# Later attention's first q and k loaded in the decode stage; the first MLP's first block in three column ranges and its residual added to the accumulator

## The chip, the cores and the metric

The kernel runs on 1 core of one Trainium2 chip. The metric is the device time of the whole program in microseconds, as the median of several runs; lower is better.

## What is computed

One layer of a hybrid decoder on a prompt of 1024 tokens and on 8 x 4 sample tokens (32 rows), model width 1024, all in float32:

```
h   = rmsnorm(x) * (1 + scale1) + shift1
q_a, k_a, v_a, q_b, f_b, i_b, g_b = split(h @ w_in)
o_a = stick_breaking(q_a, k_a, v_a)         # 8 heads x 64, strictly causal
o_b = gated linear recurrence(q_b, f_b, i_b, g_b)
x   = x + gate1 * (concat(o_a, o_b) @ w_out)
h2  = rmsnorm(x) * (1 + scale2) + shift2
x   = x + gate2 * (relu(h2 @ w_up)**2 @ w_down)
```

Stick-breaking attention gives row t the weights sigmoid(z[t,s]) * prod over s<j<t of (1 - sigmoid(z[t,j])). The sample tokens attend to 1024 cached positions each, in pages, and carry their own recurrent state.

## The kernel before, in words

Float32 products are made of three products of rounded parts: each operand is split into a high part (a cast on ScalarE) and a low part (a subtraction on VectorE or POOL), and `stationary_weights` (L202 to L204) and the down-projection (L1219 to L1221) issue high x high, high x low and low x high into one accumulation bank. Each such product has its own 128x128 weights. A weight piece is a 512 KB load on SP's queue (L159), a cast (L149) and a subtraction (L150); two raw buffers hold the loads.

The stages, in order: the start with q; k and v; the recurrence with the attention of rows 0 to 511 beside it; the first out-projection with its norm (tiles of 128 tokens, 0 to 3); the first MLP on tokens 0 to 511, with the sample tokens' decode and then the later attention (rows 512 to 1023) beside it; the second out-projection; the second MLP.

The order in which each engine gets its instructions is written at compile time by a planner. It simulates the program with its own costs; where several instructions could go, the earlier in program order goes first, moved up by the priorities that the code sets. On the chip every engine and every queue takes its instructions in that order and waits where an input isn't there. `interleave` at the end of the kernel mixes the steps of the first MLP (weight 64) with those of decode and attention (weight 166), so that the latter come earlier in program order and are at an end of their steps about halfway through the MLP's.

The first MLP (`mlp` with n = 512) goes in eight blocks of 512 hidden columns. A block's up half makes four groups of 128 hidden columns from all 512 tokens; each group is relu'd on ScalarE, squared on VectorE, cast on ScalarE and subtracted on VectorE. Its down half adds to eight accumulators `acc` of 128 tokens x 512 columns in SBUF. In the first block the up half is cut into column ranges (`CS`), so that it can start on tokens 0 to 255 while tiles 2 and 3 are still in the norm of the out-projection; ranges below column 256 use four banks (`M0`), the others two. Tile 3's norm ends with PE transposes (L314), scaling on ScalarE (L319), a cast on VectorE (L328) and a subtraction, whose second half POOL does (L329).

In the last block each piece of the down half is finished as follows: a residual tile `xres` (2 buffers, 256 KB) is loaded on SP's queue (L1231), POOL multiplies the accumulator by the gate `g2b` (L1232) and adds it to the residual (L1233), VectorE multiplies the last product by the gate (L1235) and adds it (L1236), and SP writes the result (L1237).

The decode reads 128 pages of 256 KB on SP's queue (L609 and cv's), transposes the keys on PE (L625), and at its end writes `mixs` (L691). The sample tokens' recurrence runs beside its second half; its step on PE (L996) reads kts (L988). `attention` loads for every head qh and ql (L881), kk (L882) and vhl (L884) on POOL's queue, from scratch in DRAM that is written long before. Its pool opens where the decode's pool closes, so its tiles take the addresses of the decode's. Per 128 rows: score products (L895, L896), two sigmoids (L899, L900), causal masks on POOL (L903, L904), a reversed running product on VectorE (L909), a product on POOL (L910), transposes on PE (L922), a split, and the products with v (L931, L932); at the end tv (L934, L935), written to DRAM (L936).

The second out-projection begins with products of the sample rows and the raw weights of w_out (L1097), which SP loads (L1111, L159).

Of the kernel before, what the change touches and what calls it, by code (L numbers as in the profile page):

```python
# [20 lines left out]
P = 128  # L21
# [22 lines left out]
RE = 0  # L44
CS = ((256,),(256,))
BF = dict(m="012345", y="67")
# [33 lines left out]
def hymba_step(ctx, tc, x_p, x_s, ck, cv, st_in, ptab, c_p, c_s, w_ada, b_ada, n1g, n2g, w_in,  # L80
# [787 lines left out]

    def attention(pb, ms, nbe):

        q0, nq, nk = 256 * ms[0], 256 * len(ms), 256 * (ms[-1] + 1)
        both = lambda t, part, p, r, cs: qkd[t, part, p, r, cs].unsqueeze(0).to_broadcast([2, 64, cs.stop - cs.start])
        for p in range(4):
            for hh in range(2):
                h = 2 * p + hh
                hr = slice(64 * hh, 64 * hh + 64)

                qh, ql = (pb.tile([P, nq], F32R, name=name, bufs=2) for name in ("qh", "ql"))
                kk_ = pb.tile([P, nk], F32R, name="kk", bufs=2)
                for part, tile_ in enumerate((qh, ql)):  # L880
                    G.dma_start(tile_, both(0, part, p, hr, slice(q0, q0 + nq)))  # L881
                G.dma_start(kk_, qkd[1, :, p, hr, 0:nk])  # L882
                vhl = pb.tile([P, nk // P, P], F32R, name="vhl", bufs=2)
# [285 lines left out]
    def mlp(h_hi, h_lo, t0, chunks, fp, nx, side=iter(())):  # L1169
# [5 lines left out]
        if n > 512:  # L1175
            res_s = fp.tile([NS, D], F32, name="res_s")
            nc.sync.dma_start(res_s, x1d[T:TA, :])
        else:
            g2b = fp.tile([P, D], F32, name="g2b")
        acc = [lp.tile([P, HW], F32, name=f"acc{c}", tag="acc", bufs=8) for c in range(KT)]  # L1180
        for blk in range(NBLK):
            u_hi, u_lo, ws = [], [], []
            cuts = (0,) + CS[t0 > 0] + (n,)
            parts = [slice(*x) for x in zip(cuts, cuts[1:])] if blk == 0 else chunks
# [9 lines left out]
            for m in range(NK):  # L1194
                ws.append(piece([wview(w_up, 0, KT, blk * FB_ + m * P, P)], KT, P, G if m in GL else V))
                u_hi.append(lp.tile([P, HW], F32R, name=f"uh{m}", tag="u", bufs=8))
                u_lo.append(lp.tile([P, HW], F32R, name=f"ul{m}", tag="u", bufs=8))
                if blk:
                    for cs in parts:
                        up(m, cs)  # L1200
                    next(side, None)
                    yield
            if blk == 0:
                for cs in parts:
                    for m in range(NK):
                        up(m, cs)
                    yield
            if n == 512 and blk == NBLK - 1:
                nc.sync.dma_start(g2b, g2d.to_broadcast([P, D]))
            for half_ in range(2) if n == 512 else ():  # L1210
# [3 lines left out]
                for tt in range(4):  # L1214
# [8 lines left out]
                    with tc.high_priority(offset=PV):  # L1223
# [4 lines left out]
                        else:  # L1228

                            xr = fp.tile([P, 512], F32, name="xres", tag="xres", bufs=nx)  # L1230
                            nc.sync.dma_start(xr, x1d[ts, cc])  # L1231
                            G.tensor_tensor(aa, aa, g2b[:, cc], op=mult)  # L1232
                            G.tensor_tensor(xr, xr, aa, op=add)  # L1233
                            yy = lp.tile([P, 512], F32, name="yy", tag="rr", bufs=2)
                            V.tensor_tensor(yy, pm, g2b[:, cc], op=mult)  # L1235
                            V.tensor_tensor(xr, xr, yy, op=add)  # L1236
                            nc.sync.dma_start(y_p[ts, cc], xr)  # L1237
                    if tt % 2:
# [56 lines left out]
    def decode_and_attention():  # L1295
        banks.update(BD)
        with ExitStack() as es:
            gd = decode(pool("decode", stack=es))
# [6 lines left out]
        with ExitStack() as es:  # L1305
            yield from attention(pool("attn1", stack=es), (2, 3), NBE)

# [59 lines left out]
```

## Time and profile before

| | |
|---|---|
| median of 3 runs | 1575.45 us (1572.76 to 1577.44) |
| the profiled execution | 1573.13 us |
| its span | 1571.4 us, 26224 instructions |
| PE busy | 1522.4 us, 97% |
| VectorE, ScalarE, POOL busy | 980.1, 623.9, 356.2 us |
| mean granted clock of PE | 0.988 |
| DMA | 223.14 MB, mean 142 GB/s |

The span is the time from the first to the last instruction of one profiled execution; the rows of the trace count from its start. The granted clock is a share of 2.4 GHz. A number in brackets behind a row of a timeline is the time for which the engine sat idle before it, and what ended that. PE is the product engine, PEld its weight loads, DVE VectorE, ACT ScalarE, SPq the queue of SP.

### The profile page before, as it was taken

What the parts mean: (1) busy time and instruction counts of PE and PEld (TensorE: products, weight loads), DVE (VectorE), ACT (ScalarE), POOL (GpSimd) and SP (SyncE); (2) the same over time, 40 slices, a digit from 0 to 9 for tenths busy, and PEclk for the clock granted to TensorE, in tenths of its full rate; (3) what the DMA queues carried; (4) which work ended last, traced back from release to release, by engine and by line L of the source; (5) the groups of instructions that cost most, each with busy time, mean ns of one, the idle gap of its engine ahead of it and who ended that gap; (6) DMA issues with size and microseconds to landing.
All of it is one profiled execution on the core that took longest, in us unless ns stands there. A gap on an engine that the chain in (4) does not pass through costs nothing.

```text
span 1571.4 us, 26224 instructions
## 1 busy us (share of the span) xinstructions
PE 1522.4 (97%) x9629; PEld 1276.1 (81%) x9629; DVE 980.1 (62%) x2084; ACT 623.9 (40%) x1187; POOL 356.2 (23%) x568
## 2 busy tenths in 40 slices
PE   7999999999999989999998999999899999999998
PEld 3666689998998777765566788888479999999998
DVE  4976438888866862444544977887585344444445
ACT  3742244444423453432232665655345322233330
POOL 0200125544210120000111776793110000000000
PEclk8999999999999989999998999999999999999999
DMA  9389873533124466667465374642744222322221
GB/s 327 110 282 308 259 216 67 111 65 76 50 62 143 135 193 216 204 220 248 150 153 126 98 139 99 137 117 90 234 149 146 87 89 87 94 82 86 89 82 58
DMA packets 249413, 223.14 MB, mean 142 GB/s; under 512 B 60507, under 2 KB 196259, under 8 KB 247236
## 3 DMA queue, kind: packets, MB, share of 16 engines
q1 hardware_dynamic: 186308, 199.26, 40.4%
q0 software_dynamic: 62976, 22.20, 8.4%
q8 instruction: 76, 1.25, 0.3%
q14 instruction: 53, 0.43, 0.1%
HBM read 190.14 MB, written 31.11 MB: 141 GB/s over the span
## 4 chain that ended last, share of the span: by engine, by line
PE 81%; DVE 8%; DMA 6%; issue 2%; ACT 2%; POOL 1%; SPq 0%; POOLq 0%; ACTq 0%; DVEq 0%
PE pm L202 15%; PE pm L203 15%; PE pm L204 15%; PE pm_qkv L215 3%; PE pm L1219 3%; PE pm_qkv L213 3%; PE pm_qkv L214 3%; PE pm L1221 3%; PE pm L1220 3%; PE pod L675 2%; PE ptd L625 2%; DMA wraw<-in_w_up_dram 1%; PE ptw L922 1%; DVE om L909 1%; PE pm_o L1143 1%
## 5 line engine op out<-in xcount | busy, mean ns | idle before, releaser
L202 PE MATMUL pm<-h_hi,whi 128*128 128x288 f32 (+3 forms) x1184 | 384.3, 326 | 4.9 <-DVE gg L792 1.7
L203 PE MATMUL pm<-h_lo,whi 128*128 128x288 f32 (+3 forms) x1184 | 381.9, 323 | 0.3 <-DVE h_lo L329 0.2
L204 PE MATMUL pm<-h_hi,wlo 128*128 128x288 f32 (+3 forms) x1184 | 380.9, 322 | 0.0
L149 ACT CAST whi<-wraw 128x1024 fp32r<-128x1024 f32 x160 | 167.9, 1052 | 317.9 <-PE pm L203 211.5
L150 DVE TENSOR_TENSOR wlo<-wraw,whi 128x1024 fp32r<-128x1024 f32 x144 | 185.1, 1286 | 157.5 <-ACT whi L149 151.6
L202 PEld LDWEIGHTS pm<-h_hi,whi 128*128 128x128 f32 x1184 | 223.6, 189 | 27.0 <-issue 9.8
L204 PEld LDWEIGHTS pm<-h_hi,wlo 128*128 128x128 f32 x1184 | 224.0, 189 | 10.3 <-issue 1.2
L203 PEld LDWEIGHTS pm<-h_lo,whi 128*128 128x128 f32 x1184 | 223.8, 189 | 9.6 <-DVE h_lo L329 0.9
L203 PE MATMUL pm<-ul,whi 128*128 128x256 f32 (+1 forms) x512 | 145.7, 288 | 0.0
L204 PE MATMUL pm<-uh,wlo 128*128 128x256 f32 (+1 forms) x512 | 145.5, 288 | 0.0
L202 PE MATMUL pm<-uh,whi 128*128 128x256 f32 (+1 forms) x512 | 143.7, 289 | 0.0
L909 DVE TENSOR_TENSOR_SCAN om<-om 128x128 f32<-128x128 f32 (+3 forms) x96 | 110.1, 1151 | 27.1 <-POOL om L903 18.8
L150 POOL TENSOR_TENSOR wlo<-wraw,whi 128x1024 fp32r<-128x1024 f32 x16 | 38.5, 2406 | 389.6 <-ACT whi L149 344.1
L910 POOL TENSOR_TENSOR be<-be,om 128x384 f32<-128x384 f32 (+3 forms) x96 | 100.2, 1053 | 51.5 <-DVE om L909 45.2
L1219 PE MATMUL pm<-whi,uh 128*128 128x512 f32 x256 | 106.1, 415 | 2.4 <-DVE acc L1227 2.2
L1221 PE MATMUL pm<-whi,ul 128*128 128x512 f32 x256 | 103.1, 406 | 1.6 <-DVE ul L1192 1.6
L1220 PE MATMUL pm<-wlo,uh 128*128 128x512 f32 x256 | 102.4, 401 | 0.0
L204 PEld LDWEIGHTS pm<-uh,wlo 128*128 128x128 f32 x512 | 95.9, 188 | 0.0
L203 PEld LDWEIGHTS pm<-ul,whi 128*128 128x128 f32 x512 | 95.9, 188 | 0.0
L202 PEld LDWEIGHTS pm<-uh,whi 128*128 128x128 f32 x512 | 94.6, 188 | 0.1
L1250 DVE TENSOR_TENSOR acc<-acc,pm 128x256 f32<-128x256 f32 (+1 forms) x96 | 41.0, 436 | 69.2 <-PE pm L204 69.2
L215 PE MATMUL pm_qkv<-whi,h_lo 128*128 128x512 f32 x192 | 77.6, 405 | 0.8 <-DVE h_lo L329 0.8
(354 smaller groups left out, 2860.9 us busy)
## 6 DMA issues: line engine op xcount, KB each, us to landing
wraw<-in_w_up_dram SPq DMA_DIRECT2D x64, 512.0 KB, 4.0
wraw<-in_w_down_dram SPq DMA_DIRECT2D x64, 512.0 KB, 4.8
wada<-in_w_ada_dram SPq DMA_DIRECT2D x16, 1024.0 KB, 9.1
raw<-in_cache_k_dram SPq DMA_DIRECT2D x64, 256.0 KB, 3.3
vt<-in_cache_v_dram SPq DMA_DIRECT2D x64, 256.0 KB, 3.9
wraw<-in_w_in_dram SPq DMA_DIRECT2D x24, 512.0 KB, 5.7
wa<-in_w_ada_dram SPq DMA_DIRECT2D x16, 512.0 KB, 6.4
qkd<-th SPq DMA_DIRECT2D x16, 256.0 KB, 7.1
```

The lines of the kernel that those rows point to most:

```text
L149: (V.tensor_copy if h is V else S.copy)(hi, src)
L150: (e or V).tensor_tensor(lo, src, hi.bitcast(F32), op=sub)
L202: TE.matmul(pm, w_hi[:, k, :], r_hi[k][:, cs], start=(k == 0), stop=False)
L203: TE.matmul(pm, w_hi[:, k, :], r_lo[k][:, cs], start=False, stop=False)
L204: TE.matmul(pm, w_lo[:, k, :], r_hi[k][:, cs], start=False, stop=(k == nk - 1))
L213: TE.matmul(pm, h_hi[:, k, cs], hi, start=(k == 0), stop=False)
L215: TE.matmul(pm, h_lo[:, k, cs], hi, start=False, stop=(k == KT - 1))
L909: V.tensor_tensor_scan(back, back, back, 1.0 if right is None else right[:, 0:1], op0=mult, op1=ALU.bypass)
L910: G.tensor_tensor(be[:, 0:w], be[:, 0:w], om[:, 1:w + 1], op=mult)
L1219: TE.matmul(pm, u_hi[m][:, ts], hi, start=(m == 0), stop=False)
L1220: TE.matmul(pm, u_hi[m][:, ts], lo, start=False, stop=False)
L1221: TE.matmul(pm, u_lo[m][:, ts], hi, start=False, stop=(m == NK - 1))
```

## The change

The first head's qh, ql and kk of the later attention are allocated in the pool of the first MLP, in the two buffers of the residual tiles and the one of the gate, and are loaded on POOL's queue at the start of the decode stage; vhl stays where it was. The first block of the first MLP has the column ranges 0 to 256, 256 to 384 and 384 to 512 in place of 0 to 256 and 256 to 512; the steps for the interleaving stay the same in number. In the last block the gate's load comes at the block's beginning, and after each of its four groups of the up half two residual tiles are loaded and two accumulators are multiplied by the gate and given the residual, both on POOL; the down half then multiplies by the gate and adds to the accumulator on VectorE, and writes the accumulator out.

```diff
--- before.py
+++ after.py
@@ -42,7 +42,7 @@
 PARTS = [(0,7),(7,8)]
 PN, PN0, KO = 200,1,1
 RE = 0
-CS = ((256,),(256,))
+CS = ((256,384),(256,))
 BF = dict(m="012345", y="67")
 PY = 100
 XB, NU0, NU1, EQ = "r",2,4,1
@@ -866,20 +866,27 @@
         with tc.high_priority(offset=PH):
             norm()
 
-    def attention(pb, ms, nbe):
+    def load_qk(qh, ql, kk, h, q0, nq, nk):
+
+        hr = slice(64 * (h % 2), 64 * (h % 2) + 64)
+        for part, x in enumerate((qh, ql)):
+            G.dma_start(x, qkd[0, part, h // 2, hr, q0:q0 + nq].unsqueeze(0).to_broadcast([2, 64, nq]))
+        G.dma_start(kk, qkd[1, :, h // 2, hr, 0:nk])
+
+    def attention(pb, ms, nbe, first=None):
 
         q0, nq, nk = 256 * ms[0], 256 * len(ms), 256 * (ms[-1] + 1)
-        both = lambda t, part, p, r, cs: qkd[t, part, p, r, cs].unsqueeze(0).to_broadcast([2, 64, cs.stop - cs.start])
         for p in range(4):
             for hh in range(2):
                 h = 2 * p + hh
                 hr = slice(64 * hh, 64 * hh + 64)
 
-                qh, ql = (pb.tile([P, nq], F32R, name=name, bufs=2) for name in ("qh", "ql"))
-                kk_ = pb.tile([P, nk], F32R, name="kk", bufs=2)
-                for part, tile_ in enumerate((qh, ql)):
-                    G.dma_start(tile_, both(0, part, p, hr, slice(q0, q0 + nq)))
-                G.dma_start(kk_, qkd[1, :, p, hr, 0:nk])
+                if h == 0 and first:
+                    qh, ql, kk_ = first
+                else:
+                    qh, ql = (pb.tile([P, nq], F32R, name=name, bufs=2) for name in ("qh", "ql"))
+                    kk_ = pb.tile([P, nk], F32R, name="kk", bufs=2)
+                    load_qk(qh, ql, kk_, h, q0, nq, nk)
                 vhl = pb.tile([P, nk // P, P], F32R, name="vhl", bufs=2)
                 G.dma_start(vhl, vd[0:nk, P * h:P * (h + 1)].rearrange("(t p) x -> p t x", p=P))
                 for m in ms:
@@ -1175,11 +1182,13 @@
         if n > 512:
             res_s = fp.tile([NS, D], F32, name="res_s")
             nc.sync.dma_start(res_s, x1d[T:TA, :])
-        else:
-            g2b = fp.tile([P, D], F32, name="g2b")
         acc = [lp.tile([P, HW], F32, name=f"acc{c}", tag="acc", bufs=8) for c in range(KT)]
         for blk in range(NBLK):
             u_hi, u_lo, ws = [], [], []
+            gated = n == 512 and blk == NBLK - 1
+            if gated:
+                g2b = fp.tile([P, D], F32, name="g2b", tag="g2b")
+                nc.sync.dma_start(g2b, g2d.to_broadcast([P, D]))
             cuts = (0,) + CS[t0 > 0] + (n,)
             parts = [slice(*x) for x in zip(cuts, cuts[1:])] if blk == 0 else chunks
 
@@ -1198,15 +1207,21 @@
                 if blk:
                     for cs in parts:
                         up(m, cs)
+
+                    for i in (2 * m, 2 * m + 1) if gated else ():
+                        cc, aa = slice(512 * (i // 4), 512 * (i // 4 + 1)), acc[i][:, 0:512]
+                        xr = fp.tile([P, 512], F32, name="xres", tag="xres", bufs=nx)
+                        nc.sync.dma_start(xr, x1d[P * (i % 4):P * (i % 4 + 1), cc])
+                        G.tensor_tensor(aa, aa, g2b[:, cc], op=mult)
+                        G.tensor_tensor(aa, aa, xr, op=add)
                     next(side, None)
                     yield
             if blk == 0:
                 for cs in parts:
                     for m in range(NK):
                         up(m, cs)
-                    yield
-            if n == 512 and blk == NBLK - 1:
-                nc.sync.dma_start(g2b, g2d.to_broadcast([P, D]))
+                    if cs.start != 256:
+                        yield
             for half_ in range(2) if n == 512 else ():
 
                 cc = slice(512 * half_, 512 * (half_ + 1))
@@ -1226,15 +1241,10 @@
                         elif blk < NBLK - 1:
                             V.tensor_tensor(aa, aa, pm, op=add)
                         else:
-
-                            xr = fp.tile([P, 512], F32, name="xres", tag="xres", bufs=nx)
-                            nc.sync.dma_start(xr, x1d[ts, cc])
-                            G.tensor_tensor(aa, aa, g2b[:, cc], op=mult)
-                            G.tensor_tensor(xr, xr, aa, op=add)
                             yy = lp.tile([P, 512], F32, name="yy", tag="rr", bufs=2)
                             V.tensor_tensor(yy, pm, g2b[:, cc], op=mult)
-                            V.tensor_tensor(xr, xr, yy, op=add)
-                            nc.sync.dma_start(y_p[ts, cc], xr)
+                            V.tensor_tensor(aa, aa, yy, op=add)
+                            nc.sync.dma_start(y_p[ts, cc], aa)
                     if tt % 2:
                         yield
             for c in range(KT) if n > 512 else ():
@@ -1294,6 +1304,9 @@
 
     def decode_and_attention():
         banks.update(BD)
+        first = [rp.tile([P, n], F32R, name=name, tag=tag, bufs=b)
+                 for name, n, tag, b in (("qh0", 512, "xres", 2), ("ql0", 512, "xres", 2), ("kk0", T, "g2b", 1))]
+        load_qk(*first, 0, 512, 512, T)
         with ExitStack() as es:
             gd = decode(pool("decode", stack=es))
             for _ in range(33):
@@ -1303,7 +1316,7 @@
             yield from side_by_side((gd, 28), (hgrn_decode(pool("hgrn_s", stack=es)), W[4]))
         banks.update(BA)
         with ExitStack() as es:
-            yield from attention(pool("attn1", stack=es), (2, 3), NBE)
+            yield from attention(pool("attn1", stack=es), (2, 3), NBE, first)
 
     def h2_tiles():
         return hp2.tile([P, KT, HW], F32R, name="h2_hi", tag="h2_hi", bufs=1), hp2.tile([P, KT, HW], F32R, name="h2_lo", tag="h2_lo", bufs=1)
```

## Rows read from the trace of the kernel before

**Rows 1.** Busy shares of the engines, whole page (busy us, share, instructions).
```profile
PE 1522.4 (97%) x9629; PEld 1276.1 (81%) x9629; DVE 980.1 (62%) x2084; ACT 623.9 (40%) x1187; POOL 356.2 (23%) x568
```

**Rows 2.** The chain of waits, PE's own: what, releaser, us in total, times, longest.
```profile
PE pm_os L1097 <- DMA woraw<-in_w_out_dram: 6.7, 2, 6.4
PE pz L895 <- DMA kk<-qkd: 5.0, 1, 5.0
```

**Rows 3.** Windows: stretch, length, busy us per engine, PE clock, DMA share, GB/s.
```profile
556.90:560.70 3.80, 0.00 (x0) 0.02 (x1) 3.58 (x17) 1.75 (x5) 0.00 (x0) 0.93 0.78 299
560.70:570.40 9.70, 8.34 (x36) 7.65 (x37) 5.12 (x11) 4.75 (x17) 4.82 (x13) 0.50 0.10 27
826.90:832.10 5.20, 0.15 (x2) 0.06 (x1) 0.00 (x0) 0.00 (x0) 0.00 (x0) 0.78 0.21 58
832.10:840.60 8.50, 8.30 (x23) 5.98 (x24) 4.31 (x7) 1.72 (x4) 3.74 (x7) 0.53 0.95 165
1106.60:1112.90 6.30, 0.00 (x0) 0.00 (x0) 2.44 (x4) 0.00 (x0) 2.48 (x2) 0.75 0.85 280
1112.90:1116.40 3.50, 3.45 (x12) 1.03 (x14) 2.38 (x4) 2.16 (x3) 0.00 (x0) 0.50 1.10 330
1018.00:1080.00 62.00, 61.28 (x326) 51.00 (x325) 53.64 (x60) 39.45 (x73) 51.07 (x61) 1.00 0.40 106
```

**Rows 4.** Timeline at the decode's end, all engines: start, us, operation [idle before].
```profile
813.47 1.07 SPq L159 DMA_DIRECT2D wraw<-in_w_up_dram  x1
...
832.07 0.44 PE L895 MATMUL pz<-kk,qh 128*128 128x128 f32 x1 [5.05 <-DMA kk<-qkd]
...
832.21 1.05 ACT L149 CAST whi<-wraw 128x1024 fp32r<-128x1024 f32 x1 [8.41 <-DMA wraw<-in_w_up_dram]
...
833.16 0.25 ACT L988 COPY kts<-pks 32x128 f32<-32x128 f32 x1
...
833.77 0.78 POOL L881 DMA_DIRECT2D ql<-qkd  x1 [17.78 <-DMA mixs<-ms]
```

**Rows 5.** DMA queues from 806 to 834: packets, MB, share of 16 engines.
```profile
q0 software_dynamic: 5264, 1.98, 46.1%
```

**Rows 6.** Timeline of PE at 547 and at 890.
```profile
546.92 1.04 PE L314 MATMUL ptx<-ident,xr 128*128 128x128 f32 x8
547.72 0.36 PE L203 MATMUL pm<-h_lo,whi 128*128 128x256 f32 x1
547.92 0.28 PE L204 MATMUL pm<-h_hi,wlo 128*128 128x256 f32 x1
548.04 0.29 PE L202 MATMUL pm<-h_hi,whi 128*128 128x256 f32 x1
...
889.88 0.22 PE L931 MATMUL pv<-wh,vhl 128*128 128x128 f32 x1
889.94 0.44 PE L1220 MATMUL pm<-wlo,uh 128*128 128x512 f32 x1
```

**Rows 7.** Timeline of ScalarE at the decode's start.
```profile
580.16 1.05 ACT L149 CAST whi<-wraw 128x1024 fp32r<-128x1024 f32 x1 [1.70 <-DMA wraw<-in_w_down_dram]
```

**Rows 8.** Costliest groups, the residual's two: count, busy and mean, idle before.
```profile
L1233 POOL TENSOR_TENSOR xres<-xres,acc 128x512 f32<-128x512 f32 x8 | 11.7, 1476 | 25.1 <-DMA xres<-x1d 25.0
...
L1236 DVE TENSOR_TENSOR xres<-xres,yy 128x512 f32<-128x512 f32 x8 | 7.4, 950 | 8.1 <-POOL xres L1233 8.1
```

**Rows 9.** Timelines of POOL, PE, ScalarE, VectorE, SP at the block's end.
```profile
1077.70 1.36 POOL L910 TENSOR_TENSOR be<-be,om 128x512 f32<-128x512 f32 x1 [1.25 <-ACT whi L149]
...
1095.32 0.49 PE L922 MATMUL ptw<-ident,be 128*128 128x128 f32 x3
...
1102.11 0.37 ACT L934 COPY tv<-pv 64x256 f32<-64x256 f32 x1 [3.71 <-PE pv L932]
...
1105.75 0.41 DVE L935 TENSOR_TENSOR tv<-pv,tv 64x256 f32<-64x256 f32 x1
...
1108.34 0.90 SPq L1111 DMA_DIRECT2D woraw<-in_w_out_dram  x2
```

## The prediction

> **What bounds the kernel now.** I read the busy shares first, then what TensorE (PE) waited for, then a table of busy times for the stretches around its longest waits, then those stretches instruction by instruction on every engine. PE is busy 1522.4 us of a span of 1571.4 [rows 1], so 49 us of idle time is all that a better order could give back, besides the time in which PE runs at its lower clock. Of the waits two stand out: 6.7 us on the output projection's weights and 5.0 us on the first kk of the later attention [rows 2]. The table [rows 3] shows three holes and what follows each. From 556.9 to 560.7 PE does nothing while tile 3 of the first out-projection is normalised; then the granted clock is 0.50, which is 1.2 GHz of 2.4, until 570.4, and 8.34 of those 9.7 us are busy. From 826.9 to 832.1 it does 0.15 us of work, and 8.30 busy us at 0.53 follow. From 1106.6 to 1112.9 it does none, and 3.45 busy us at 0.50 follow. Each idle hole is followed by a stretch at the lower level, and a busy microsecond there is worth about half a microsecond at the full one. So the first hole costs 3.8 + 1.4 + 8.34/2 = 9.3 us, the second 5.2 + 0.2 + about 3.9 = 9.3, the third 6.3 + 3.45/2 = 8.0. The three parts of the change lie one at each hole.
>
> **Part 1, first q and k early.** The wait on kk ends at 832.07, but other things end there too [rows 4]: the up-projection weights that SP issued at 813.47 reach ScalarE only at 832.21 (it sat idle 8.41 us), the copy kts queued behind that cast on ScalarE runs at 833.16, and PE's next work after the four score products is the product that reads kts. On POOL, the second head's ql waits 17.78 us for the write of mixs, until 833.77, and the first head's masks are queued behind it. If only kk came earlier, the four products would move forward and the hole would stay: gain 0. What can move the end is traffic. In this stretch the software queue moved 1.98 MB and took 46.1% of the DMA engines [rows 5]; qh, ql and kk (256, 256 and 512 KB by their shapes) are half of it, and they now move to the start of the decode stage. Against that, the next head's loads can move into the place left empty, since the pool now places vhl first and the others elsewhere. Ends: 0, if the weights land as late as before, and 9.3, if the hole and the slow stretch go. I see no row nearer to one end, so I take the middle: **-4.5**. Two other stalls come next in line: the weights cast and kts.
>
> The three loads are not free where they go. They are three issues of about 0.78 us each (the ql row in [rows 4]), 2.3 us on POOL at the start of the decode stage, ahead of the memsets for the decode's queries, and 1 MB of traffic beside the first cache pages and down weights. There a cast already waited 1.70 us for w_down [rows 7]. PE has up products to run meanwhile; without that cover the whole 2.3 us of issue would show, and 1 MB at 280 GB/s (the third hole's rate in [rows 3]) keeps the DMA engines 3.7 us. Taken: **+1**, ends 0 and +4. Buffers: qh0, ql0 and kk0 sit in those of the residual and gate tiles, which are wanted only in the last block; they are free after one head of eight, so I put no cost there.
>
> **Part 2, three column ranges.** The second range (tiles 2 and 3, 96 products of 256 columns) becomes two of 128, 192 products. Range 256 to 384 needs only tile 2, so it can fill the first hole. The price is what a 128-column product costs when each has its own 128x128 weights. A 256-column product follows its predecessor after 0.12 us (547.92 to 548.04) [rows 6]. The nearest row to a run of 128-column ones is the run of eight transposes, 128 columns with own weights each: 1.04 us from first start to last end, 0.80 to the next product's start, so 0.10 to 0.13 each; I take 0.11. A lone one between long products leaves 0.06 to the next start, but that next one (512 columns) then lasts 0.44 [rows 6], so part of its weight load shows. Before: 96 x 0.12 = 11.5 plus the hole's 9.3. After, with the hole filled: 192 x 0.11 = 21.1. Sum: 21.1 - 11.5 - 9.3 = **+0.3**, nothing gained. Ends: at 0.06 each, 11.5 - 20.8 = -9.3; at 0.13 each, +4.2. The range also makes 12 evictions of 4 from 8, on ScalarE and VectorE, hidden under PE, which has 24 x 0.11 = 2.6 us of products per 128-column bank. A copy of 256 columns took ScalarE 0.37 [rows 9]; four steps for each of four more evictions would be 5.9 us if that cover were gone.
> A page of the Trainium skill would make the price smaller: "TensorE: Matmul & The Clock Gate", section "Back-to-back issue gap", gives about 81 ns per product for a sustained stream of 128-column ones, each with its weights. By it 192 x 0.081 = 15.6, and this part would come to -5.2.
>
> **Part 3, residual onto the accumulator.** Now each residual tile (two buffers) is loaded, added on POOL to the gated accumulator, added by VectorE to the last product, written out, and only then is the buffer free. POOL waited 25.0 us in all for those loads, VectorE 8.1 us for POOL [rows 8]. It sets the end of the block: ScalarE has the last head's tv at 1102.11 + 0.37, VectorE adds it only at 1105.75, behind those waits, and SP issues the output projection's first weights at 1108.34, behind the residual's writes and loads [rows 9]; PE resumes 4.6 us later. After, the loads and both POOL steps are done in the up half, and at the end there is only VectorE's two operations and the write. tv can be added at about 1102.5, written at 1103.0, and the weights issued at 1103.5: 4.8 us earlier, which leaves 1.5 us of the hole. A hole that short I count at full clock: 4.8 + 1.7 = **-6.5**. Ends: -1, if the weights' new buffer waits for the last products and for tv's write, or SP has the last outputs first; -8 if all goes. The next stall then is that landing, 4.6 us after the issue.
> Moved, not added: the eight POOL adds of 1.48 us [rows 8]. Six of them ran after the attention's last POOL work; they now stand inside it, 8.9 us more on an engine busy 51.07 of 62 us there [rows 3]. The eight loads queue on SP among the weight loads, and the gate's load sits behind the first head. Cover: the attention's last POOL product ends at 1079.06 and the last transposes that read such rows start at 1095.32 [rows 9], 16.3 us of slack. Taken: **+0.5**, ends 0 and, cover gone, the third rival.
>
> **Sum.** -4.5 + 1 + 0.3 - 6.5 + 0.5 = -9.2 us. The profiled execution took 1573.13 (span 1571.4 and 1.7 around it), which gives 1563.9; the median of the runs is 2.3 higher, so I forecast **1566**.
>
> **Rivals.**
> (1) Hidden anyway: kk comes early, but PE then waits for the weights and kts to the same microsecond. For it: rows 4 show three ends within 1.7 us; against it: the halved traffic. Part 1 is 0: 1570.7. The same time comes out if part 3's new buffers cost most of its gain.
> (2) The weight loads run mostly beside the products, so 128 columns cost their columns, 0.06 each. For it the 0.06 row, against it the run of transposes. Part 2 is -9.3: 1556.6. The Trainium skill's 81 ns ("TensorE: Matmul & The Clock Gate", "Back-to-back issue gap") lies between, at 1560.7.
> (3) Slower: POOL becomes the bound of the last block. The waits for residual loads, 25.0 us in three waits now after the attention, come to stand inside it, with the masks and row products of its last heads queued behind them. Price: 25.0 + 8.9 - 16.3 = 17.6 us later for the last products, which end at 1102, so tv at about 1120, the weights 5.6 us behind it at 1125.7 against 1112.9: +12.8, with part 3's gain gone. With -3.2 from the other terms: 1585. It decides once waits and adds exceed the 16.3 us of slack. Against it: the loads have the whole up half, and two of them can be there before it.
> (4) The hole isn't filled: PE takes its queue in order, and if the planner puts tile 3's transposes ahead of the middle range's products, PE waits for them as now and pays the 96 extra products too. Part 2 is +9.6: 1575.5, no change.
>
> **How the numbers follow.** Forecast 0.45, rival 1 0.18, rival 2 0.15, rival 3 0.11, rival 4 0.11. About 0.3% (4.7 us) is what a measurement of this kernel can tell from no change: faster is below 1570.7, slower above 1580.2. Faster: 0.45 x 0.9 + half of rival 1 + rival 2 + a little of rival 4, 0.67. Slower: rival 3 and a trace of rival 4, 0.12. The rest is 0.21. The range runs from rival 2's time to just past rival 4's, 1556 to 1577; it leaves out rival 3 and the far end of rival 2.
>
> **What would show it.** Part 1: the first pz long before 832, and whether the cast of the up weights still waits until then; the clock at 832 to 840. Part 2: no idle time before tile 3's transposes, clock 1.00 throughout, and the start-to-start of the 128-column products: near 0.11 here, near 0.06 by rival 2. Part 3: VectorE no longer waits for POOL, and the first w_out load is issued within 2 us of the last tv. Wrong would be: the hole at the decode's end as long as before, POOL's masks waiting for residual loads, or PE idle before the middle range.

## The result, and the profile after

Slower by 1.0%: 1591.6 us (1588.5 to 1598.0) against 1575.0 (1572.8 to 1577.4), ratio 1.0104, 95% interval 1.0089 to 1.0120. The profiled execution took 1592.9, with a span of 1591.2. The forecast was 1566 in a range of 1556 to 1577, with a chance of 0.12 for slower. Times here are medians and ratios are of means; in three kernels with part 2 (e2, e9, e14) two executions each lie 6 to 13 us above the median at a lower mean clock, so that the two measures differ there by up to 2 us.

The page's first part answers to [rows 1]: 18 us more of busy time, 96 more products.
```profile
PE 1540.4 (97%) x9725; PEld 1290.8 (81%) x9725; DVE 983.9 (62%) x2092; ACT 626.7 (39%) x1195; POOL 359.2 (23%) x568
```
PE's waits after (what, releaser, us in total, times, longest) answer to [rows 2]:
```profile
PE pm_os L1104 <- DMA woraw<-in_w_out_dram: 6.2, 1, 6.2
PE ptd L625 <- DMA raw<-in_cache_k_dram: 5.6, 2, 4.3
PE pv L938 <- DVE tv L942: 3.5, 3, 1.8
PE pm L202 <- ACT rr L1198: 3.2, 1, 3.2
```
The kk wait is gone; the output weights' wait is as long as it was; new are the decode's cache pages (raw) and a wait for ScalarE.

Windows after (columns as in [rows 3]):
```profile
556.90:560.70 3.80, 2.68 (x25) 2.54 (x24) 3.57 (x18) 1.52 (x5) 0.00 (x0) 1.00 0.78 300
576.90:584.20 7.30, 1.67 (x9) 1.52 (x8) 2.77 (x6) 2.21 (x5) 0.00 (x0) 0.69 0.92 204
592.00:596.00 4.00, 4.00 (x20) 4.00 (x20) 1.43 (x2) 1.22 (x2) 0.00 (x0) 0.50 0.10 31
580.00:600.20 20.20, 17.65 (x79) 15.61 (x80) 4.58 (x10) 4.49 (x9) 0.00 (x0) 0.50 0.56 150
826.90:832.10 5.20, 5.20 (x26) 3.75 (x25) 3.86 (x9) 2.30 (x6) 3.77 (x6) 1.00 0.92 172
1124.20:1130.40 6.20, 0.05 (x1) 0.00 (x0) 1.61 (x3) 0.17 (x1) 0.00 (x0) 0.91 0.57 183
```
Read them against the three holes. The first is mostly filled, at full clock. The second is gone. The third is there unchanged, 18 us later. And there is a new one at 577 to 584 with a stretch at half clock until 600. Its timeline (POOL, SP, PE, ScalarE; start, us, operation, idle before):
```profile
566.42 0.90 POOL L873 DMA_DIRECT2D qh<-qkd  x1
567.32 0.81 POOL L873 DMA_DIRECT2D ql<-qkd  x1
568.12 0.79 POOL L874 DMA_DIRECT2D kk<-qkd  x1
...
577.26 0.39 SPq L159 DMA_DIRECT2D wraw<-in_w_down_dram  x1
...
581.26 1.09 PE L625 MATMUL ptd<-ident,raw 128*128 128x128 f32 x4 [4.34 <-DMA raw<-in_cache_k_dram]
582.00 0.46 PE L203 MATMUL pm<-h_lo,whi 128*128 128x128 f32 x1
...
584.17 1.09 PE L625 MATMUL ptd<-ident,raw 128*128 128x128 f32 x4 [1.29 <-DMA raw<-in_cache_k_dram]
...
593.02 1.05 ACT L149 CAST whi<-wraw 128x1024 fp32r<-128x1024 f32 x1 [9.86 <-DMA wraw<-in_w_down_dram]
...
599.75 0.67 PE L1234 MATMUL pm<-whi,uh 128*128 128x512 f32 x1
```
Down weights issued at 577.26 are cast at 593.02; before, a load issued at 574.67 was cast at 580.16 [rows 7]. At the end of that wait the DMA engines were nearly empty: 31 GB/s at 592 to 596. PE itself waits here only for the two pages, 5.6 us in all. The up products stood behind the first page in its order, and from 582 on it works through them at half clock: 17.65 busy us at 0.50 between 580 and 600, by an estimate half of them, 8.8, due to the clock. The DMA view of after, 566 to 590 (KB each, median us from issue to landing):
```profile
kk<-qkd POOLq DMA_DIRECT2D x1, 512.0 KB, 23.6
...
qh<-qkd POOLq DMA_DIRECT2D x1, 256.0 KB, 9.0
ql<-qkd POOLq DMA_DIRECT2D x1, 256.0 KB, 13.1
s0b<-in_state_hgrn_dram POOLq DMA_DIRECT2D x4, 64.0 KB, 19.7
```
The states of 64 KB (s0b), issued behind kk, landed 2.3 us after their issue in the kernel before and 19.7 after it here.

Where the time went, by three events of the timelines and the span (start in us, in brackets the shift against the kernel before). "down" is the first block's first down product, "sqos" ScalarE's step behind the write of the states, "pm_os" the output projection's first product:

| kernel | down | sqos | pm_os | span |
|---|---|---|---|---|
| before | 583.6 | 853.8 | 1113.0 | 1571.4 |
| after | 599.8 (+16.1) | 865.3 (+11.5) | 1130.5 (+17.5) | 1591.2 (+19.8) |
| e2, part 2 alone | 586.2 (+2.6) | 856.8 (+3.0) | 1116.9 (+3.9) | 1575.0 (+3.6) |
| e3, part 3 alone | 581.6 (-2.1) | 857.4 (+3.6) | 1122.4 (+9.4) | 1581.4 (+10.0) |
| e8, part 3, no steps | 583.7 (+0.1) | 859.8 (+5.9) | 1113.6 (+0.7) | 1575.6 (+4.2) |
| e9, first loads halved | 585.6 (+2.0) | 854.3 (+0.5) | 1121.9 (+9.0) | 1582.1 (+10.7) |
| e15, part 1, two heads halved | 581.2 (-2.5) | 852.2 (-1.6) | 1113.5 (+0.5) | 1571.7 (+0.3) |
| e17, before, two heads halved | 583.7 (+0.1) | 840.1 (-13.8) | 1106.7 (-6.2) | 1567.8 (-3.6) |

So the change loses 16.1 at the decode's start, gets 4.6 back by the decode's end, loses 6.0 from there to pm_os and 2.3 in the final stage (the last not looked into).

### The profile page after: what moved, and what is told of

Same layout as the page of the kernel before. It is cut to its first block, busy times and chain, and to the rows that moved or that the text cites. A ratio compares the mean times of both kernels' runs of the same rounds, so it can differ in the third digit from the quotient of the medians.

```text
span 1591.2 us, 26414 instructions
## 1 busy us (share of the span) xinstructions
PE 1540.4 (97%) x9725; PEld 1290.8 (81%) x9725; DVE 983.9 (62%) x2092; ACT 626.7 (39%) x1195; POOL 359.2 (23%) x568
## 4 chain that ended last, share of the span: by engine, by line
PE 80%; DVE 7%; DMA 5%; issue 3%; POOL 2%; ACT 1%; SPq 0%; DVEq 0%; POOLq 0%; ACTq 0%
PE pm L202 14%; PE pm L204 14%; PE pm L203 14%; PE pm L1234 3%; PE pm L1236 3%; PE pm_qkv L215 3%; PE pm L1235 3%; PE pm_qkv L213 3%; PE pm_qkv L214 3%; PE pod L675 2%; PE ptd L625 2%; PE ptw L929 2%; DVE om L916 1%; PE pzd L631 1%; PE pada L264 1%
## 5 line engine op out<-in xcount | busy, mean ns | idle before, releaser
L202 PE MATMUL pm<-h_hi,whi 128*128 128x288 f32 (+4 forms) x1216 | 393.6, 324 | 6.5 <-ACT rr L1198 3.2
L203 PE MATMUL pm<-h_lo,whi 128*128 128x288 f32 (+4 forms) x1216 | 391.6, 322 | 0.1
L204 PE MATMUL pm<-h_hi,wlo 128*128 128x288 f32 (+4 forms) x1216 | 391.1, 322 | 0.0
L202 PEld LDWEIGHTS pm<-h_hi,whi 128*128 128x128 f32 x1216 | 230.5, 190 | 30.1 <-issue 11.5
L204 PEld LDWEIGHTS pm<-h_hi,wlo 128*128 128x128 f32 x1216 | 231.5, 190 | 10.3 <-issue 1.2
L203 PEld LDWEIGHTS pm<-h_lo,whi 128*128 128x128 f32 x1216 | 231.1, 190 | 9.0 <-DVE h_lo L329 0.3
L916 DVE TENSOR_TENSOR_SCAN om<-om 128x128 f32<-128x128 f32 (+3 forms) x96 | 115.8, 1210 | 30.2 <-POOL om L910 23.1
```

Of the source, the lines that this page charges most:

```text
L202: TE.matmul(pm, w_hi[:, k, :], r_hi[k][:, cs], start=(k == 0), stop=False)
L203: TE.matmul(pm, w_hi[:, k, :], r_lo[k][:, cs], start=False, stop=False)
L204: TE.matmul(pm, w_lo[:, k, :], r_hi[k][:, cs], start=False, stop=(k == nk - 1))
L916: V.tensor_tensor_scan(back, back, back, 1.0 if right is None else right[:, 0:1], op0=mult, op1=ALU.bypass)
```

## The experiments

Ratios are to the kernel before, run on the same chip, with 95% intervals.

**e1, part 1 alone.**
```diff
-CS = ((256,384),(256,))
+CS = ((256,),(256,))
```
and the residual's hunks as before.

> Part 1 alone: the three early loads as in the change; two column ranges and the late residual as before. Theory A (the 1 MB of q and k from the software queue, issued at the decode's start, drains through one or two DMA engines for about 20 us, and the cache pages and the first down weights land behind it): a hole and a slow stretch at 575 to 600 with the first down product about 12 to 16 us later than in the kernel before, the hole at 827 gone (about 7 us back), 3 us lost again at the next wait; about +12 us, 1587. Rival B (the loss at the decode's start comes from part 2: SP has two more cache pages ahead of the first down weights, and PE has 96 more short products): no loss at the decode's start, only the gain at 827, about -4 to -7 us, 1569 to 1571.

Measured 1591.2, 1.0093 (1.0074 to 1.0112). The size is theory A's, the places are so only in part: the first down product comes 8.9 us later and not 12 to 16, with 5.6 us in three waits for pages, and PE waits 6.7 us for ScalarE until 873. Part 1 alone costs as much as the whole change.

A part of that isn't part 1's. The decode's 128 pod products (L675) are split otherwise by the planner's order. PE's groups, before and then e15 (busy us, mean ns); e1's are as e15's:
```profile
L675 PE MATMUL pod<-vt,wt 128*32 128x512 f32 x128 | 28.3, 602 | 0.0
```
```profile
L675 PE MATMUL pod<-vt,wt 128*32 128x512 f32 x128 | 32.6, 602 | 0.0
```
It is 32.6 in e1, e3, e7, e8, e11, e13, e15 and e16, and 28.3 in the whole change, e2, e9, e14, e17 and e18. So up to 4.3 us of what the former lose against the kernel before is that order. By the ratios the parts alone cost 14.6, 4.6 and 7.7 us, 27 in sum, and the whole 16.4; that order, counted in two of the three, is up to 8.6 of the difference.

**e2, part 2 alone**: the residual's hunks as before, and
```diff
-        load_qk(*first, 0, 512, 512, T)
...
-            yield from attention(pool("attn1", stack=es), (2, 3), NBE, first)
+            yield from attention(pool("attn1", stack=es), (2, 3), NBE)
```

> Part 2 alone: three column ranges, no early loads, late residual. Theory A: hole at 557 filled, no tail at 575 to 600, so between -5 and +1 us, 1570 to 1576. Rival B: the first down weights land late behind two more pages that wait for PE, first down product some 14 us later, about +14 us, 1589.

Measured 1577.7, 1.0029 (1.0008 to 1.0049): a little beyond A's range, far from B's.

**e3, part 3 alone**: e2's diff, the residual's hunks as in the change, and
```diff
-CS = ((256,384),(256,))
+CS = ((256,),(256,))
```

> Part 3 alone: residual added to the accumulator in the up half of the last block; no early loads, two ranges. Theory C (the 16 POOL steps inside the attention delay the masks and row products of its last heads, so the last pv becomes PE's last work and the output weights are issued no earlier against it): about +5 to +8 us, 1580 to 1583, with PE still idle about 6 us at the block's end. Rival D (the lateness of the attention in the changed kernel was a consequence of the other parts' shifts): tv written about 4.8 us earlier against the last product, -6.5 us as predicted, 1568.5.

Measured 1583.6, 1.0049 (1.0034 to 1.0063). C's size; but PE's hole before pm_os was gone, so the time was lost ahead of it.

**e4, loads written later in the program.**
```diff
+            for i in range(33):
+                if i == 16:
+                    load_qk(*first, 0, 512, 512, T)
```

> The whole change, with the three early loads issued after 16 of the decode's first 33 steps and not at its start (the buffers are taken at the same place). Theory A: the pages and down weights at 575 to 600 land as fast as in the kernel before, the 14 to 16 us there come back, and the hole at 827 stays gone: about 1576 (part 3's loss is still in it). Rival B: unchanged against the whole change, about 1591, first down product at about 600.

Measured 1597.7, 1.0136 (1.0117 to 1.0156), but it tells nothing of A or B: the loads wait for nothing, so they left POOL at 571 to 573 all the same. It showed something else, below: 24 us at half clock with PE busy throughout.

**e5, e7, plain loads through SP** (e5 in the whole change, e7 in part 1 alone).
```diff
-        first = [rp.tile([P, n], F32R, name=name, tag=tag, bufs=b)
+        first = [rp.tile([P, n], F32, name=name, tag=tag, bufs=b)
-        load_qk(*first, 0, 512, 512, T)
+        load_qk(*first, 0, 512, 512, T, nc.sync)
...
+                    for x, y in zip((qh, ql, kk_), first):
+                        S.copy(x, y)
```

> The whole change, but the three early loads go through SP's queue without a cast, in front of the cache pages, into plain buffers, and ScalarE casts them when the attention begins (three casts, about 2.3 us). Theory A (what holds up the pages and down weights is the cast load in the software queue, draining on one or two DMA engines, with PE's lower clock behind it): the same 1 MB costs little here, first down product within 4 us of the kernel before, no idle time of PE at 577 to 585; about 1579 to 1582, the rest being part 3. Rival A2 (the bytes themselves or PE's short products cost it, whatever queue): stays at 1588 to 1593.

> Part 1 alone with plain loads through SP's queue and ScalarE's casts, two ranges, late residual. Theory A: no loss at the decode's start; the hole at 827 gone; but PE then waits at about 862 for ScalarE, which stands behind the write of the states, so most of the gain is lost again: 1570 to 1577. If the hole at 862 does not come, 1566.

Measured 1604.3, 1.0194 (1.0176 to 1.0212), and 1603.5, 1.0190 (1.0160 to 1.0220). Both missed: the loss is there without the software queue and the cast, so these are not the cause. But e7 shows the cause bare. For 8 us no engine computes and hardly anything moves but packets of 2 to 8 KB, 101 of 107 (a row of kk has 4 KB). Windows, DMA queues and PE's waits of e7:
```profile
580.00:588.00 8.00, 0.00 (x0) 0.00 (x0) 0.00 (x0) 0.00 (x0) 0.00 (x0) 0.50 0.13 50
```
```profile
q1 hardware_dynamic: 107, 0.40, 12.6%
```
```profile
PE ptd L625 <- DMA raw<-in_cache_k_dram: 17.7, 1, 17.7
```
12.6% of sixteen engines is 2.0 engines, 50 GB/s. These loads' access patterns begin with a dimension of 2 (two parts, or a broadcast to two halves) by 64 rows. The Trainium skill has the rule, "DMA: Bandwidth & Descriptors", section "Why a DMA increments its semaphore by 16 and not by 1": the number of engines is the largest up to 16 that divides the slowest dimension (of more than 1) of both access patterns. By it these loads get two; the trace agrees with 2.0.

**e6, loads truly late.**
```diff
+            if n == 512 and blk == 2:
+                S.copy(firsts[0][0][:, 0:1], acc[7][:, 0:1])
...
+                load_qk(*firsts[0], 0, 512, 512, T)
```

> The whole change, the three early loads by the same cast loads on POOL, but each behind a one-column write that reads block 1's accumulator, so that they cannot leave POOL before the third block of the MLP (about 650 us). Theory A: decode's start as in the kernel with part 2 alone, first down product +2 to +4 us; the drain meets pages and weights that are loaded ahead, and PE stays busy: 1578 to 1583. Rival B (SP's order, with two more pages ahead of the first down weights, makes the loss): first down product still at about 600, 1591.

Measured 1589.4, 1.0119 (1.0060 to 1.0178). The loads left at 699 to 701 (kk took 24.1 us to land) and the first down product came at 587.8, +4.1: B is out. The total is above A's range and near B's 1591, though not for B's reason: sqos is at +6.0 and pm_os at +15.5, so the other losses are larger here than in e9; why wasn't settled.

**e8, part 3 without POOL's steps.**
```diff
-                        G.tensor_tensor(aa, aa, g2b[:, cc], op=mult)
-                        G.tensor_tensor(aa, aa, xr, op=add)
```

> Part 3 alone without POOL's sixteen gate and residual steps (so the residual and the gate on the accumulator are left out of the result); the residual's loads stay. Theory C (those steps on POOL delay the attention): the 5 to 6 us between the decode's end and the last pv come back, 1575 to 1578, PE's waits on wl and tv at 1020 to 1080 gone. Rival C2 (the loss comes from the changed order of SP and PE alone): stays at 1582 to 1584.

Measured 1575.0, 0.9996 (0.9984 to 1.0009): the sixteen steps are worth 8 us. Eight of them, the multiplications by the gate, ran on POOL inside the attention in the kernel before too (L1232, 1018 to 1052), so e8 takes off more than part 3 put on. PE's waits, e3 and then e8:
```profile
PE pv L939 <- DVE wl L150: 7.7, 6, 2.8
```
```profile
PE pv L939 <- DVE wl L150: 2.6, 2, 1.9
```

**e9, the whole change, its three early loads halved.**
```diff
+        for a in range(2 if q0 and h == 0 else 0):
+            o = slice(64 * a, 64 * a + 64)
+            for part, x in enumerate((qh, ql)):
+                G.dma_start(x[o], qkd[0, part, h // 2, hr, q0:q0 + nq])
+            G.dma_start(kk[o], qkd[1, a, h // 2, hr, 0:nk])
```

> The whole change; the three early loads, whose access pattern has an outermost extent of 2, are issued as six loads of 64 rows each (same bytes, same place, same queue). Theory A, now with its cause (a load with outermost extent 2 is carried by two of the sixteen DMA engines; plain loads through SP did the same: 50 GB/s at a share of 0.13, and kk over 15 us): spread over all engines the 1 MB lands in about 5 us, no wait of PE for pages at 577 to 585, first down product +3 to +6 us: 1577 to 1582. Rival A2 (the 1 MB of bytes, or PE's short products): 1588 to 1593, first down product still near 600.

Measured 1584.3, 1.0063 (1.0041 to 1.0085): 2 us above A's range, well below A2's. The place is as expected: first down product +2.0 and not +16.1, no wait for pages. A new wait came later: PE stands 4.0 us until 836.7 for an addition on VectorE, which is queued behind a mask on POOL, which is queued behind the next loads and the write of mixs. Same bytes, queue and moment (DMA view and windows of e9, to be read beside those of after):
```profile
kk<-qkd POOLq DMA_DIRECT2D x2, 256.0 KB, 4.1
...
qh<-qkd POOLq DMA_DIRECT2D x2, 128.0 KB, 3.2
ql<-qkd POOLq DMA_DIRECT2D x2, 128.0 KB, 3.4
s0b<-in_state_hgrn_dram POOLq DMA_DIRECT2D x4, 64.0 KB, 4.5
```
```profile
576.90:584.20 7.30, 7.30 (x64) 6.30 (x64) 4.50 (x17) 3.11 (x7) 0.00 (x0) 1.00 0.88 247
580.00:600.20 20.20, 20.20 (x130) 15.91 (x130) 7.62 (x16) 8.17 (x15) 0.00 (x0) 1.00 0.68 207
```

**e10, e11, e12, all sixteen heads' loads halved**, in the kernel before, in part 1 alone, in the whole change. e9's five lines for every head:
```diff
+        for a in range(2):
```

> The kernel before with nothing changed but the q and k loads of all sixteen heads of both attentions issued as halves of 64 rows. Theory A: kk lands in about 5 us and not 15, the up weights at 813 aren't held up, so the hole at 827 shrinks from 5.4 us and its slow stretch goes; three more issues a head on POOL (about 0.5 us each) cost little: 1565 to 1572. Rival A3 (the hole at 827 comes from the late issue of the second head's loads on POOL, not from the drain): 1575 to 1578.

> Part 1 alone (early loads on POOL at the decode's start, two ranges, late residual), all q and k loads as halves. Theory A: no loss at the decode's start (first down product within 3 us of the kernel before), the hole at 827 gone, and the wait for ScalarE at 862 short, since the second head's loads no longer block the write of the states: 1564 to 1571. Rival: as part 1 alone, 1587 to 1592.

> The whole change with all q and k loads as halves. Theory A: e9's time, less what the hole at 862 gives back: 1572 to 1579; what is left above the kernel before is part 3's (POOL's steps in the attention) and the 96 short products. Rival A2: 1588 or more.

Measured 1585.0, 1.0044 (1.0031 to 1.0057); 1579.6, 1.0015 (1.0006 to 1.0024); 1590.2, 1.0085 (1.0071 to 1.0098). All miss theory A; e12 lies in rival A2's range, but the halving alone costs 7 us by the ratio in e10, where the early loads and parts 2 and 3 are not in. kk landed in a median of 3.7 us in e10 (14.9 before) and the hole at 827 went, but tile 3's transposes started 9.7 us later: halving in the first attention costs that ahead of the change's place, and sqos to the last pv took another 8. POOL issues six loads of 0.55 us a head in place of three of 0.82; whether that is the cost wasn't isolated.

**e13, e15, part 1 with the first head's, or the first two heads' loads halved**: e1's diff, e9's lines, and for e15
```diff
-        for a in range(2 if q0 and h == 0 else 0):
+        for a in range(2 if q0 and h < 2 else 0):
```

> Part 1 alone, only the three early loads as halves of 64 rows (two ranges, late residual, all other loads as before). Theory A: no loss at the decode's start (first down product within 3 us of the kernel before), hole at 827 gone, a part of it lost again at 830 to 890: 1569 to 1574. If part 1 can't gain whatever its loads cost: 1575 to 1578.

> As part 1 with its early loads halved, and the later attention's second head's loads halved too (three more issues on POOL). If that head's loads, on two engines, are what holds up the write of the states and the weights at 830 to 870, 2 to 4 us less than part 1 with only the early loads halved: 1566 to 1571; if POOL's issues or other waits set it, the same within 2 us.

Measured 1585.2, 1.0056 (1.0044 to 1.0068), a miss, and 1575.6, 0.9995 (0.9986 to 1.0004): the second head's shape is worth 9 to 10 us, but part 1 comes only to nothing. e13's profiled execution, 1579.0, was its quickest, so where its other 6 us lie isn't shown. In e15 the window 826.90 to 832.10 is full at clock 1.00, and yet sqos gains only 1.6. The order of the pod products (under e1) takes up to 4.3 us of it back; the rest isn't accounted for.

**e14, parts 1 and 2, first loads halved, late residual**: e9 with the residual's hunks undone,
```diff
-                            V.tensor_tensor(aa, aa, yy, op=add)
+                            V.tensor_tensor(xr, xr, yy, op=add)
```
and what belongs to it.

> Parts 1 and 2 with the three early loads as halves, late residual as before. It differs from the whole change with the first loads halved (1584.3) by part 3 alone. Theory C: part 3's 8 to 9 us come back: 1574 to 1577, sqos near the kernel before, the last pv within 3 us of it. Rival C2 (the late attention there is of parts 1 and 2): 1582 or more.

Measured 1576.3, 1.0001 (0.9989 to 1.0012): 8.0 below e9, which is part 3. Its trace is of an execution of 1582.5, with a stretch at low clock like e4's (0.59 from 564.20 to 588.10).

**e16, part 3's steps on VectorE.**
```diff
-                        G.tensor_tensor(aa, aa, g2b[:, cc], op=mult)
-                        G.tensor_tensor(aa, aa, xr, op=add)
+                        V.tensor_tensor(aa, aa, g2b[:, cc], op=mult)
+                        V.tensor_tensor(aa, aa, xr, op=add)
```

> Part 3 alone with its sixteen gate and residual steps on VectorE and not on POOL. Theory C in its narrow form (POOL is what they delay, with the masks and row products queued behind them): VectorE, 50 of 60 us busy there too, takes 16 x 0.69 us, so part of the loss comes back: 1576 to 1580. If it is the steps' work on either engine between the attention's steps: 1582 to 1588.

Measured 1579.5, 1.0024 (1.0013 to 1.0035): about half of e3's loss comes back, and 4.5 us remain above e8. So both: POOL is the worse place, and the work costs on either engine.

**e17, e18, the kernel before, nothing moved, the later attention's first two heads (e18: the first) halved.** e9's lines with
```diff
+                for a in range(2 if q0 and h < 2 else 0):
```
(`h < 1` in e18).

> The kernel before, nothing of the change, but the q and k loads of the later attention's first two heads as halves of 64 rows. Theory A: kk and the up weights land some 5 us earlier at 822 to 832 and the hole there shrinks: 1568 to 1573, the least of all kernels here. If the gain at that place is always taken back by the wait behind the write of the states and by the order of the products, as with part 1 done the same way: 1574 to 1577.

> As the kernel before, with only the first head's loads of the later attention as halves. Theory A: the first head's kk comes about 5 us earlier, but the second head's loads still run on two engines beside the weights: 1571 to 1575, between the kernel before and the one with two heads halved.

Measured 1566.4, 0.9932 (0.9918 to 0.9947), and 1566.8, 0.9943 (0.9923 to 0.9962): both beat the kernel before and the change, and both by more than expected. The up weights and kts, at 832.21 and 833.16 in [rows 4], and the second hole of [rows 3], in e17 (timeline of ScalarE, window):
```profile
824.27 1.05 ACT L149 CAST whi<-wraw 128x1024 fp32r<-128x1024 f32 x1 [0.35 <-PE pm L1227]
825.22 0.25 ACT L994 COPY kts<-pks 32x128 f32<-32x128 f32 x1
```
```profile
826.90:832.10 5.20, 5.20 (x27) 3.94 (x26) 2.82 (x6) 0.63 (x2) 2.29 (x5) 1.00 1.22 243
```
The hole at the decode's end was the two-engine loads' own; the change had moved their traffic to a place where it cost more. With the same two heads' loads in halves, the kernel that also moves the first head's (e15) is 9 to 10 us slower than the one that moves nothing (e17); up to 4.3 of these are the pod order. The table's row of e17 is from its slowest execution, 1569.5.

## Why the prediction was wrong, step by step

Two steps failed: the price of the early loads, and part 3's cover. By the medians (of different chips) the forecast is 25.6 us too low: 7.3 are the early loads' shape (the change less e9), 14.0 are part 3 (e9 less e14 is +8.0, where -6.0 was forecast), and 4.3 are parts 1 and 2 with the loads in halves (e14).

**Part 1, the price of the early loads: the first step that failed.** "Taken: +1, ends 0 and +4", from 2.3 us of issue and "1 MB at 280 GB/s ... 3.7 us". The issue was as priced (0.90, 0.81 and 0.79). The rate was not: it is that of transfers on all engines, and these loads run on two. At the 50 GB/s of e7, 1 MB would take about 21 us, an estimate. e9 changes the shape and keeps bytes, queue and place: 14.1 us at the first down product (16.1 less 2.0), 8.5 at pm_os. The cover named, PE's up products, didn't cover: at 577 a cache page that hadn't landed came first in PE's order, with the up products behind it, and after the wait they ran at half clock. The kernel before showed it. These are lines of its views by tile, kk and then wraw, both 512 KB at most:
```profile
DMA to landing us min/median/max: 9.8/14.9/19.0
```
```profile
DMA to landing us min/median/max: 3.4/4.2/9.2
```
And the second hole of [rows 3] stands there at a DMA share of 0.21 and 58 GB/s. The prediction took the traffic of the whole stretch (46.1%) and passed over this low share inside the hole, which was a long transfer on few engines.

**Part 1's gain, -4.5.** "What can move the end is traffic" was right in kind: e17 moves nothing and closes the hole by shape alone. In the change the hole closed too, and 3.2 us came back at 868, where ScalarE waits 8.33 us for the states' write ahead of PE's eviction. In e15, with good loads, part 1 comes to nothing: rival 1's size, by another way than it said. As the pod order stands against it there, what part 1 is worth by itself stays open.

**Part 2, +0.3.** The terms hold at their place: 0.11 us per 128-column product, and the hole filled but for 1.1 us. Timeline of PE after, at full and at half clock:
```profile
569.08 0.28 PE L203 MATMUL pm<-h_lo,whi 128*128 128x128 f32 x1
569.19 0.28 PE L204 MATMUL pm<-h_hi,wlo 128*128 128x128 f32 x1
...
588.08 0.41 PE L202 MATMUL pm<-h_hi,whi 128*128 128x128 f32 x1
588.29 0.41 PE L203 MATMUL pm<-h_lo,whi 128*128 128x128 f32 x1
```
The sum was too low: e2 gives 1.0029, some 4.6 us (1.3 to 7.7), by medians 2.6, and its first down product +2.6. The upper end was +4.2. Rival 2's 0.06 and rival 4's unfilled hole didn't come; nor did the Trainium skill's 81 ns ("TensorE: Matmul & The Clock Gate", "Back-to-back issue gap"), and the measurement decides. What had no term: the short products take 0.21 us each at the low clock, and after the new hole the clock was 0.50 for the last of them.

**Part 3, -6.5 and +0.5: the second step that failed.** The first mechanism is real: in e8 PE no longer waits for the output weights (6.4 us before), and sqos to pm_os takes 253.9 us against 259.1 before, -5.3. e8 gains nothing in all, since sqos comes 5.9 later there; the pod order is up to 4.3 of that. The second term failed: "slack 16.3 us ... +0.5". With the steps sqos to pm_os takes 265.0 (e3), 11.1 more than without them, and 8.6 of it is left between the medians. In the whole change it is the attention that gets longer: from sqos to its last pv 248.0 us before, 248.8 in e14 (without part 3), 260.0 in e9 and 258.4 after. Rival 3 had the place and the sign, but not the way: in the changed kernel POOL waited only 1.1 us for a residual load (25.0 in [rows 8]). It is the steps themselves, 16 of about 1.3 us, between the attention's own; the prediction counted the six additions that part 3 brought in there, 8.9 us, but set them against slack at the attention's end. In the whole change the last pv then ends PE's block, so the weights are late against it as before:
```profile
1123.80 0.45 PE L1236 MATMUL pm<-whi,ul 128*128 128x512 f32 x1
...
1124.90 0.41 DVE L942 TENSOR_TENSOR tv<-pv,tv 64x256 f32<-64x256 f32 x1
...
1125.33 0.48 SPq L943 DMA_DIRECT2D mixa<-tv  x1
...
1126.53 1.18 SPq L1118 DMA_DIRECT2D woraw<-in_w_out_dram  x2
...
1130.48 1.06 PE L1104 MATMUL pm_os<-woraw,smp_k 128*32 128x512 f32 x1 [6.22 <-DMA woraw<-in_w_out_dram]
```
tv is added 1.1 us after PE's last start and the issue follows 1.6 later, nearly as forecast; but only that one down product follows the last pv (1123.69), where before 4.3 us of them did.

## What to carry to other kernels

Before a transfer is priced by its bytes, compare its landing time with that of a load of the same size: 14.9 us beside 4.2 was the sign here that it ran on few engines, and its shape, not its place, was what to change. A hole in which the DMA share is small but not zero can be such a transfer's tail; here, moving the load moved the hole. Slack read on an engine's last instruction is not slack for work put between its earlier ones. And where a planner orders the instructions, a part measured alone carries its own order with it: look whether groups that the edit doesn't touch (here pod) stay as they were.

## What was not expected of the hardware

A run of 128-column products stayed at the low clock for 24 us with PE never idle. Windows of e4 and e2, the same stretch of the same products, each after one wait of 1.1 us:
```profile
564.20:588.10 23.90, 23.90 (x117) 23.90 (x115) 9.23 (x37) 7.99 (x27) 9.46 (x20) 0.50 0.34 74
```
```profile
564.20:588.10 23.90, 23.90 (x198) 21.73 (x198) 16.16 (x45) 11.02 (x31) 7.07 (x17) 1.00 0.66 203
```
PE has no idle time in either; e4 does 117 products where e2 does 198. In the kernel before the stretch at 0.50 behind the first hole was 9.7 us long [rows 3]. What decides whether the clock falls after that short wait isn't settled; the prediction, which counted a hole of 1.5 us at full clock, had no row for it.

The decode's pod products overlap: in e15 a group of two lasts as long as one of six, so an order that splits them costs (28.3 and 32.6 us, under e1). Timeline of PE in e15:
```profile
708.98 1.06 PE L675 MATMUL pod<-vt,wt 128*32 128x512 f32 x6
712.02 1.05 PE L675 MATMUL pod<-vt,wt 128*32 128x512 f32 x2
```
